# Attention's output projection in three columns at a time, its weights laid out in order of use, and new tables of turns

## The chip, the cores and the metric

The kernel runs on one core of one Trainium2 chip. The metric is device time in microseconds (us), the median of several runs. Matrix products run on TensorE (PE, with its weight loads shown as PEld), elementwise work on VectorE (DVE), ScalarE (ACT) and GpSimd (POOL); SyncE (SP), ACT and POOL also issue DMAs.

## The reference: a GLA layer, an attention layer, a gated MLP behind each

512 tokens of width 1024 go through two layers. Layer 0 mixes tokens by gated linear attention, layer 1 by softmax attention; a gated MLP with a width-3 convolution follows each. The change is in layer 1's mixer:

```python
def attn_mixer(h, w_qkv, q_norm, k_norm, w_out, cos, sin):
    ...
    q = apply_rope(rmsnorm(q, q_norm).astype(jnp.float32), cos, sin).astype(h.dtype)
    k = apply_rope(rmsnorm(k, k_norm).astype(jnp.float32), cos, sin).astype(h.dtype)
    ...
    def block(q_blk):
        s = jnp.einsum('bkgqd,bksd->bkgqs', q_blk, k).astype(jnp.float32) * scale
        p = jax.nn.softmax(s, axis=-1).astype(v.dtype)
        return jnp.einsum('bkgqs,bksd->bkgqd', p, v)
    o = lax.map(block, qb)
    o = o.transpose(1, 0, 4, 2, 3, 5).reshape(B, S, ATTN_Q_HEADS * ATTN_HEAD_DIM)
    return o @ w_out
```

There are 8 query heads and 2 key/value heads of 128; queries go in blocks of 128. The output o (512 x 1024) is multiplied by w_out (1024 x 1024) and added to x.

## The kernel before

Activations lie feature-major: x is eight tiles x[c] of 128 features x 512 tokens. Products keep float32 precision by splitting each operand into a high part and a low rest (tiles `wh`, `wl` of weights, the two halves of `xhl`, `q`, `k`, `oT`): `mm3` (line 385) issues high x high, high x low and low x high into one PSUM bank. PSUM's eight banks are pools by tag: three `acc`, two `s`, two `pt`, one `po`.

**Weights.** A class `Weights` holds a list of halves in order of use. `get` converts the next half ahead of time: SP loads 1 MB into one of two `raw` buffers, ACT copies it to `wh` (line 167), and either DVE subtracts (line 172) or ACT writes minus the high part to `wl` (line 169) and a POOL DMA adds the raw weights onto it (line 210). The `w` pool has six tiles, three halves. The first four of the eight halves of `w_aout` go by POOL's DMA, the other four by DVE.

**The turns.** The attention part works on 32 blocks (head h, query block j), one per turn t of the loop at the end of `attention`; "turn t" below is the turn in which block t's scores are issued. Turn t issues:

- `scores` of block t: 3 matmuls of 512 columns into an `s` bank, DVE's maximum `mx` (line 1060) and `nb` (line 1061), ACT's exponential `p` with its sum `sm` (line 1063);
- `copy` of block t-1: an ACT-queue DMA `pr<-p` (line 1075);
- pieces of other work that the table names for this turn;
- `turn` of block t-LAG: four PE transposes into a `pt` bank (line 1087), ACT's high part `pth` (line 1090), DVE's rest `ptl` (line 1091), which frees the bank;
- `shares` of block t: DVE's reciprocal `rc` (line 1068), ACT's scaling of `p` (line 1069);
- in every second turn `mix`, two blocks back by LAG2: 12 matmuls of 256 columns (`po`) from `pth`, `ptl` and v; after a head's second mix, `oT` is split by ACT and DVE (lines 980, 981).

LAG and LAG2 are 5 and 7. The other work has two sources. `qpair(i)`, i = 1 to 3, makes heads 2i and 2i+1: 16 steps of 3 matmuls (tiles A and B), squares (`qa`, `qb`), four rotations `rt` on DVE, a tiny product `hs` on PE whose DVE result POOL raises to a power (`qsc`), sums `ry` on POOL, and the split of `q`. `out_steps` is the output projection: for a pair of columns c it walks the heads k in steps of 6 matmuls, alternating between the two columns' banks. It does heads 0 to 5 for columns 0, 1 (`acc`) and 2, 3 (`s`), heads 6 and 7 for these, and then columns 4, 5 and 6, 7 whole. A finished column is added to x (line 449) and prepared for the MLP by `nxt.chunk`, which writes an `xhl` tile. That pool has eight tiles, and the `oT` of heads 4 to 7 lie in it too. Twelve of the 32 steps are issued in turns, from turn 22 on; the others follow the loop.

The framework then orders instructions on each engine by priority, starting from this order of issue, and assigns banks and semaphores; each engine runs its own list strictly in order. The tables therefore decide where on PE's list a piece stands between the parts of the softmax chain.

Of the kernel before, what the change touches and what calls it, by code (L numbers as in the profile page):

```python
# [13 lines left out]
ALU = mybir.AluOpType  # L14

P = 128
S = 512
D = 1024
KC = D // P
# [10 lines left out]

GATE_STEPS, GATE_LAG = (0, 2, 5, 7, 10, 12, 15, 17), 2

LAGS = (5, 7)

Q_STEPS = {1: (0, (4,) * 4), 2: (4, (3, 3, 2, 2, 2, 2, 2)), 3: (11, (2,) * 8)}
Q_READY = {1: (4, (3, 3, 2, 1, 1, 0, 1)), 2: (11, (3, 2, 2, 1, 1, 1, 0, 1)), 3: (19, (3, 2, 2, 1, 1, 1, 0, 1))}

O_STEPS = (22, 23, 25, 27, 29, 31, 32, 33, 34, 35, 36, 37)


PLAIN = 6
PARTS = (4, 4, 4, 4, 3, 3)
TILES = {4: (2, 2, 2, 2), 3: (2, 3, 3)}
# [16 lines left out]
def hybrid_encoder_kernel(  # L60
# [21 lines left out]
    pe, act, dve, pool, sync = nc.tensor, nc.scalar, nc.vector, nc.gpsimd, nc.sync  # L82
    pinned = [False]

    def mm(*a, **k):
        i = pe.matmul(*a, **k)  # L86
        if pinned[0]:
            tc.keep_in_program_order(i)
# [13 lines left out]
    def bank(tag, n):  # L102
        return pp.tile([P, S], F32, tag=tag, bufs=PS[tag], name=nm(n))
# [17 lines left out]
    x = [cp.tile([P, S], F32, name=f"x{c}") for c in range(KC)]  # L121
# [112 lines left out]
    W = Weights()  # L234
# [191 lines left out]
    def out_steps(src, hl, nxt):  # L426


        pss, ws = {}, {}

        def part(ng, ks):
            if ng not in pss:
                pss[ng] = [bank("s" if ng % 2 else "acc", "op") for _ in range(2)]
            for k in ks:
                hf, kk = divmod(k, 4)
                if (ng, hf) not in ws:
                    ws[ng, hf] = W.half(src, ng * 2 + hf)
                wh, wl = ws[ng, hf]
                for i, (wt, mv) in enumerate(((wh, hl[k][0]), (wh, hl[k][1]), (wl, hl[k][0]))):
                    for n in range(2):  # L440
                        sl = slice((kk * 2 + n) * P, (kk * 2 + n + 1) * P)
                        mm(pss[ng][n], wt[:, sl], mv, start=k == 0 and i == 0, stop=k == KC - 1 and i == 2)
                W.flush()
                yield

        def end(ng):
            for n in range(2):
                c = ng * 2 + n
                dve.tensor_tensor(x[c], x[c], pss[ng][n], ALU.add)
                nxt.chunk(c)  # L450

        yield from part(0, range(6))
        yield from part(1, range(6))
        for ng in range(2):
            yield from part(ng, (6, 7))
            end(ng)
        for ng in (2, 3):
            yield from part(ng, range(KC))
            end(ng)


    def gla(norm, nxt):
        norm.high(0)
# [451 lines left out]
    def attention(norm, nxt):  # L915
# [90 lines left out]
        def qpair(i, tag="acc"):  # L1006
            head, sc = yield from roped(1 + i, PC_QK, float(HD), "qsc", tag)
            for e in range(2):
                y = head(e)
                yield  # L1010
                t = big(F32R, "q")
                split(y, t)
                heads[2 * i + e] = (t, sc, e)
                yield
# [18 lines left out]
        ps = [bank("acc" if j < 2 else "pt", "av") for j in range(NT)]  # L1033
# [8 lines left out]
        for j in range(NT):  # L1042
            sl = slice(j * 256, (j + 1) * 256)
# [4 lines left out]
        oh = [None] * QH  # L1048
# [57 lines left out]

        LAG, LAG2 = LAGS
        blocks = [(h, j) for h in range(QH) for j in range(NT)]
        osteps = out_steps(w_aout, oh, nxt)
        plan = collections.defaultdict(list)  # L1110
        for i in range(1, QH // 2):
            g = qpair(i)
            for first, counts in (Q_STEPS[i], Q_READY[i]):
                for t, n in enumerate(counts):
                    plan[first + t] += [g] * n
        for t in O_STEPS:
            plan[t].append(osteps)
        for t in range(len(blocks) + LAG2):
            if t < len(blocks):
# [29 lines left out]
    with staged("att"):  # L1149
        attention(norms[2], norms[3])  # L1150
# [4 lines left out]
def _layout(inputs):  # L1155

    import numpy as np

    i = {k: np.asarray(v) for k, v in inputs.items()}
    con = np.ascontiguousarray  # L1160
    a = {}
    a["xT"] = con(i["x"][0].T)
    fm = lambda w: w.reshape(-1, P).T
    q, k = i["attn_q_norm"][0], i["attn_k_norm"][0]
    dup = lambda w: np.concatenate([w, w])[:, None]
    a["par"] = con(np.concatenate(
        [fm(i["norm_mix"][0]), fm(i["norm_ffn"][0]), fm(i["norm_mix"][1]), fm(i["norm_ffn"][1]),
         fm(i["gla_b_gate_f"][0]), fm(i["gla_b_gate_b"][0]),
         dup(q[:64]), dup(q[64:]), dup(k[:64]), dup(k[64:])], axis=1))
    cv = np.concatenate([i["ffn_w_conv"], i["ffn_b_conv"][:, None, :]], axis=1)  # L1170
    a["conv"] = con(cv.reshape(2, 4, 2 * FC, P).transpose(3, 0, 2, 1).reshape(P, -1))
    a["gla_norm"] = con(np.broadcast_to(i["gla_norm"][0], (P, DV)))
    wg = np.zeros((32, 1024), np.float32)
    wg[:16, :512] = i["gla_w_gate_up_f"][0]
    wg[16:, 512:] = i["gla_w_gate_up_b"][0]
    a["w_gate"] = wg
    inv = (10000.0 ** (-np.arange(32) / 32)).astype(np.float32)
    row = np.repeat(np.arange(8, dtype=np.float32), 64)
    col = np.tile(np.arange(64, dtype=np.float32), 8)
    ang = np.concatenate([row[:, None] * inv, col[:, None] * inv], axis=1).T.astype(np.float64)  # L1180
    ang = np.concatenate([ang, ang])
    a["rope"] = con(np.concatenate([np.cos(ang), np.sin(ang)], axis=1).astype(np.float32))
    sm = np.ones((P, S + 1), np.float32)
    sm[:, ::CHUNK] = 0.0
    a["scan_mask"] = sm

    w = i["gla_w_in"][0]
    ks = lambda m: m.reshape(m.shape[0] // P, P, -1)
    vg = ks(w[:, 1024:3072]).reshape(2, 4, P, 4, S)
    a["w_vg"] = con(vg.transpose(3, 0, 2, 1, 4).reshape(8, P, 4 * S))  # L1190
    a["w_r"] = con(ks(w[:, 3072:]).transpose(1, 0, 2).reshape(P, KC * 32))
    qk = ks(w[:, :1024]).reshape(KC, P, 2, GH, P)[:, :, ::-1]
    a["w_kq"] = con(qk.transpose(3, 1, 2, 0, 4).reshape(GH, P, 4 * S))

    def outw(m):
        return con(ks(m).reshape(KC, P, 4, 2, P).transpose(2, 1, 0, 3, 4).reshape(4, P, 4 * S))

    a["w_gout"] = outw(i["gla_w_out"][0])
    w = i["attn_w_qkv"][0]

    def halves(m):
        n = m.shape[1] // 256
        t = m.reshape(KC, P, n, 2, 2, 64)
        return t.transpose(2, 1, 4, 0, 3, 5).reshape(n, P, 4 * S)

    a["w_akq"] = con(np.concatenate([halves(w[:, 1024:1280]), halves(w[:, :1024])]))
    a["w_av"] = con(ks(w[:, 1280:]).transpose(1, 0, 2).reshape(1, P, 4 * S))
    a["w_aout"] = outw(i["attn_w_out"][0])
    up = i["ffn_w_up"].reshape(2, KC, P, 2, FC, P)
    a["w_up"] = con(up.transpose(0, 4, 2, 3, 1, 5).reshape(2, FC, P, 4 * S))  # L1210
    dn = i["ffn_w_down"].reshape(2, FC, P, KC, P)
    ends = np.cumsum((0,) + PARTS)
    dn = np.concatenate([dn[:, a:b].transpose(0, 3, 1, 2, 4).reshape(2, -1, P, P) for a, b in zip(ends, ends[1:])], axis=1)
    dn = dn.reshape(2, KC * FC // 16, 16, P, P)
    a["w_down"] = con(dn.transpose(0, 1, 3, 2, 4).reshape(2, -1, P, 4 * S))
    return a
# [19 lines left out]
```

## Time and profile before

| | |
|---|---|
| median of 3 runs | 1117.07 us (1115.98 to 1118.34) |
| profiled execution | 1119.08 us, span 1117.4 us |
| PE busy | 1104.9 us, 99% of the span, 6418 matmuls |
| DVE, ACT, POOL busy | 864.3, 601.0, 105.9 us |
| attention part with its turns, in the trace | about 590 to 764 us |

A busy share of PE counts each matmul from its start to its modelled end, and neighbours overlap; so short holes vanish in it, and starts have to be compared. Waits are shown by the line that waited and what released it.

### The profile page before, as it was taken

What the parts mean: (1) busy time and instruction counts of PE and PEld (TensorE: products, weight loads), DVE (VectorE), ACT (ScalarE), POOL (GpSimd) and SP (SyncE); (2) the same over time, 40 slices, a digit from 0 to 9 for tenths busy, and PEclk for the clock granted to TensorE, in tenths of its full rate; (3) what the DMA queues carried; (4) which work ended last, traced back from release to release, by engine and by line L of the source; (5) the groups of instructions that cost most, each with busy time, mean ns of one, the idle gap of its engine ahead of it and who ended that gap; (6) DMA issues with size and microseconds to landing.
All of it is one profiled execution on the core that took longest, in us unless ns stands there. A gap on an engine that the chain in (4) does not pass through costs nothing.

```text
span 1117.4 us, 16142 instructions
## 1 busy us (share of the span) xinstructions
PE 1104.9 (99%) x6418; PEld 974.1 (87%) x6418; DVE 864.3 (77%) x1325; ACT 601.0 (54%) x892; POOL 105.9 (9%) x96
## 2 busy tenths in 40 slices
PE   9999999999999999999999999999999999999998
PEld 7878888888899999999978887788879999999997
DVE  6566655459989999979885567654998999997985
ACT  6455224367645455544464788845764545544541
POOL 0213310021000000000004332101100000000000
PEclk9999999999999999999999999999999999999999
DMA  6323211368332322323337754446863232332322
GB/s 219 128 78 111 76 40 37 113 140 198 135 113 95 113 92 98 115 74 114 136 76 200 180 164 117 152 127 145 191 173 114 96 113 81 109 114 76 114 76 76
DMA packets 30938, 131.78 MB, mean 118 GB/s; under 512 B 3600, under 2 KB 4240, under 8 KB 22160
## 3 DMA queue, kind: packets, MB, share of 16 engines
q1 hardware_dynamic: 20496, 102.30, 27.5%
q0 software_dynamic: 5472, 19.93, 9.2%
q10 hardware_dynamic: 4896, 8.54, 2.1%
q8 instruction: 50, 0.82, 0.3%
q14 instruction: 24, 0.20, 0.1%
HBM read 100.34 MB, written 2.10 MB: 92 GB/s over the span
## 4 chain that ended last, share of the span: by engine, by line
PE 91%; DMA 3%; DVE 3%; ACT 2%; issue 1%; POOL 0%; SPq 0%; DVEq 0%; POOLq 0%; ACTq 0%
PE dn L86 20%; PE Y L86 16%; PE X L86 12%; PE up L86 9%; PE op L86 8%; PE vg L86 5%; PE A L86 3%; PE B L86 2%; PE po L86 2%; PE k L86 2%; PE q L86 2%; PE s L86 2%; DMA wl<-raw 2%; PE o L86 2%; PE av L86 1%
## 5 line engine op out<-in xcount | busy, mean ns | idle before, releaser
L86 PE MATMUL dn<-gu,wh 128*128 128x512 f32 x708 | 218.5, 390 | 0.8 <-DVE x L842 0.7
L86 PEld LDWEIGHTS dn<-gu,wh 128*128 128x128 f32 x708 | 130.4, 188 | 26.8 <-DVE x L842 2.1
L86 PE MATMUL dn<-gu,wl 128*128 128x512 f32 x354 | 137.4, 388 | 0.0
L86 PE MATMUL up<-xhl,wh 128*128 128x512 f32 x384 | 118.7, 390 | 0.0
L776 ACT ACTIVATE y<-u,cw 128x512 f32<-128x512 f32 x88 | 67.9, 808 | 78.4 <-DVE u L876 64.2
L167 ACT ACTIVATE wh<-raw 128x1024 fp32r<-128x1024 f32 x72 | 76.2, 1058 | 60.7 <-DVE raw L199 15.3
L86 PE MATMUL X<-th,xwh 128*128 128x256 f32 x360 | 101.9, 283 | 0.0
L86 PE MATMUL X<-th,xwl 128*128 128x256 f32 x360 | 101.9, 283 | 0.0
L86 PE MATMUL X<-tl,xwh 128*128 128x256 f32 x360 | 101.9, 283 | 0.0
L842 DVE TENSOR_TENSOR x<-x,dn 128x512 f32<-128x512 f32 x95 | 64.7, 684 | 27.9 <-PE dn L86 27.7
L167 ACT ACTIVATE wh<-draw 128x1024 fp32r<-128x1024 f32 x44 | 46.7, 1061 | 70.5 <-PE dn L86 35.5
L86 PEld LDWEIGHTS up<-xhl,wh 128*128 128x128 f32 x384 | 71.8, 188 | 14.7
L86 PE MATMUL vg<-wh,xhl 128*128 128x512 f32 x256 | 81.9, 398 | 1.4 <-DVE g L485 0.5
L210 POOL DMA_DIRECT2D wl<-raw x38 | 33.4, 878 | 515.0 <-ACT wl L169 508.7
L86 PEld LDWEIGHTS dn<-gu,wl 128*128 128x128 f32 x354 | 66.5, 188 | 13.8
L86 PE MATMUL up<-xhl,wl 128*128 128x512 f32 x192 | 75.0, 391 | 0.9 <-DMA wl<-raw 0.8
L86 PE MATMUL Y<-th,wh 128*128 128x256 f32 x264 | 74.7, 283 | 0.0
L86 PE MATMUL Y<-tl,wh 128*128 128x256 f32 x264 | 74.7, 283 | 0.0
L86 PE MATMUL Y<-th,wl 128*128 128x256 f32 x264 | 74.7, 283 | 0.0
L86 PE MATMUL op<-oT,wh 128*128 128x512 f32 x256 | 72.2, 395 | 0.0
L86 PEld LDWEIGHTS X<-th,xwh 128*128 128x128 f32 x360 | 69.0, 192 | 0.8 <-DVE v L856 0.7
L86 PEld LDWEIGHTS X<-tl,xwh 128*128 128x128 f32 x360 | 69.1, 192 | 0.1
(232 smaller groups left out, 2810.9 us busy)
## 6 DMA issues: line engine op xcount, KB each, us to landing
raw<-in_w_up_dram SPq DMA_DIRECT2D x44, 1024.0 KB, 5.0
draw<-in_w_down_dram SPq DMA_DIRECT2D x44, 512.0 KB, 3.8
wl<-raw POOLq DMA_DIRECT2D x38, 512.0 KB, 5.8
pr<-p ACTq DMA_DIRECT2D x32, 256.0 KB, 2.9
raw<-in_w_vg_dram SPq DMA_DIRECT2D x6, 1024.0 KB, 5.0
raw<-in_w_akq_dram SPq DMA_DIRECT2D x5, 1024.0 KB, 6.6
raw<-in_w_kq_dram SPq DMA_DIRECT2D x4, 1024.0 KB, 4.9
raw<-in_w_gout_dram SPq DMA_DIRECT2D x4, 1024.0 KB, 4.9
```

The source lines that it names most:

```text
L86: i = pe.matmul(*a, **k)
L167: act.activation(hi, r, AF.Copy)
L210: pool.dma_start(dst, src, accum_op=ALU.add)
L776: act.activation(yt, ut, AF.Identity, scale=w(1), bias=w(3))
L842: dve.tensor_tensor(x[c], x[c], ps, ALU.add)
```

## The change

The change replaces the two lags and all tables of turns, and gives the attention layer's output projection a generator of its own, `out_stream`. Its unit is one block of 128 x 128 weights: one head k, one column c, 3 matmuls in a row on one bank. `out_blocks` lists the 64 units: heads 0 to 5 for columns 0 to 2 (`acc`), head by head; heads 0 to 5 for column 3, then 4 (`s`); heads 6 and 7 for columns 0 to 2, then for 3 and 4; last columns 5, 6, 7, one after the other. The layout of `w_aout` in memory follows the list, 8 units to a half, so that each half is read once from front to back. A column is added to x and handed to `nxt.chunk` as soon as it is complete. The GLA layer keeps `out_steps`. The lists of SP and POOL stay as they were; PE still has the same number of matmuls, ACT and DVE the same instructions in another order.

```diff
-LAGS = (5, 7)
-
-Q_STEPS = {1: (0, (4,) * 4), 2: (4, (3, 3, 2, 2, 2, 2, 2)), 3: (11, (2,) * 8)}
...
-O_STEPS = (22, 23, 25, 27, 29, 31, 32, 33, 34, 35, 36, 37)
+LAGS = (4, 5)
+
+Q_AT = {1: (2, 2, 2, 2, 2, 2, 2, 2, 2, 2, 2, 2, 3, 3, 3, 3, 4, 4, 4, 5, 5, 5, 6, 6, 7, 8, 10),
...
+O_AT = (18, 18, 18, 18, 19, 22, 22, 23, 23, 26, 27, 28, 29, 32, 32, 32, 32, 33, 37, 37, 37, 37, 37, 37, 38, 38, 38, 38, 38, 38)
...
+    def out_blocks():
+
+        first, second, third = range(3), range(3, 5), range(5, KC)
+        return ([(k, c) for k in range(6) for c in first] + [(k, c) for c in second for k in range(6)]
+                + [(k, c) for k in (6, 7) for c in first] + [(k, c) for c in second for k in (6, 7)]
+                + [(k, c) for c in third for k in range(KC)])
+
+    def out_stream(src, hl, nxt):
+        ps, w = {}, None
+        for u, (k, c) in enumerate(out_blocks()):
+            if u % 8 == 0:
+                w = W.half(src, u // 8)
+            if c not in ps:
+                ps[c] = bank("s" if 3 <= c < 5 else "acc", "op")
+            sl = slice((u % 8) * P, (u % 8 + 1) * P)
+            mm3(ps[c], w[0][:, sl], w[1][:, sl], *hl[k], k == 0, k == KC - 1)
+            W.flush()
+            if k == KC - 1:
+                dve.tensor_tensor(x[c], x[c], ps[c], ALU.add)
+                nxt.chunk(c)
+            yield
...
-        osteps = out_steps(w_aout, oh, nxt)
+        osteps = out_stream(w_aout, oh, nxt)
         plan = collections.defaultdict(list)
         for i in range(1, QH // 2):
             g = qpair(i)
-            for first, counts in (Q_STEPS[i], Q_READY[i]):
-                for t, n in enumerate(counts):
-                    plan[first + t] += [g] * n
-        for t in O_STEPS:
+            for t in Q_AT[i]:
+                plan[t].append(g)
+        for t in O_AT:
             plan[t].append(osteps)
```

PE's list, turns 27 and 28 and the start of turn 29, before: `s_6631`, `s_6662` and `s_6698` are the scores of these three turns, `op` is the projection, `oT` a head's output.

```order
L86 MATMUL s_6631<-k_5411,q_6501 128x512 x3
L1087 MATMUL pt_6653<-ident,pr_6499 128x128 x4
L86 MATMUL s_6662<-k_5411,q_6604 128x512 x3
L1087 MATMUL pt_6676<-ident,pr_6533 128x128 x4
L86 MATMUL op_6450<-oT_6628,wh_6452 128x512
L86 MATMUL op_6451<-oT_6628,wh_6452 128x512
L86 MATMUL s_6698<-k_5411,q_6604 128x512
```

The same place now, from turn 27's scores `s_6673`; eight more rows of this mix, four transposes and the scores of turn 28 follow.

```order
L84 MATMUL s_6673<-k_5411,q_6495 128x512 x3
L84 MATMUL op_6337<-oT_6603,wh_6333 128x512
L84 MATMUL op_6337<-oT_6603,wl_6334 128x512
L84 MATMUL op_6342<-oT_6603,wh_6333 128x512
L84 MATMUL po_6660<-pth_6580,vh_5565 128x256
L84 MATMUL op_6342<-oT_6603,wl_6334 128x512
L84 MATMUL op_6346<-oT_6603,wh_6333 128x512
L84 MATMUL op_6346<-oT_6603,wl_6334 128x512
L84 MATMUL po_6660<-ptl_6581,vh_5565 128x256
L84 MATMUL po_6660<-pth_6580,vl_5566 128x256
```

Turn 27 held one group of transposes between two scores; it now holds six projection matmuls and a whole mix. Over turns 18 to 30 the list before has 39 `s`, 30 `op`, 2 B, 84 `po`, 13 groups of four transposes and one `hs`; now 39 `s`, 48 `op`, 72 `po`, 13 groups and one `hs`. On ACT the same turns hold 13 times the chain's three instructions, four weight conversions, `qa` and `qb` both times, and of `q` and `oT` splits 7 before and 5 now.

DVE's list around the last `hs`, that of `qpair(3)`, before; `rc_6376` belongs to turn 20, `mx_6411` to turn 21.

```order
L954 SCALAR_TENSOR_TENSOR rt_6346<-A_6015,prm,rope_5235 128x512
L933 SCALAR_TENSOR_TENSOR hs_6354<-hs_6349,eps 128x8
L954 SCALAR_TENSOR_TENSOR rt_6345<-B_6016,prm,rope_5235 128x512
L1068 RECIPROCAL rc_6376<-sm_6375 128x1
L1060 TENSOR_REDUCE mx_6411<-s_6407 128x1
```

And now; `rc_6384` belongs to turn 19, `mx_6418` to turn 20.

```order
L974 SCALAR_TENSOR_TENSOR rt_6330<-A_6018,prm,rope_5235 128x512
L953 SCALAR_TENSOR_TENSOR hs_6396<-hs_6391,eps 128x8
L974 SCALAR_TENSOR_TENSOR rt_6329<-B_6019,prm,rope_5235 128x512
L1111 TENSOR_TENSOR ptl_6354<-pt_6355,pth_6353 128x4x128
L974 SCALAR_TENSOR_TENSOR rt_6331<-B_6019,prm,rope_5235 128x512
L1088 RECIPROCAL rc_6384<-sm_6383 128x1
L1080 TENSOR_REDUCE mx_6418<-s_6414 128x1
```

The reciprocal behind `hs` has two instructions more in front of it, and belongs to a turn earlier. On PE the product `hs` that it waits for stood behind the scores of turn 21, and now stands behind those of turn 20.

More of the change, by code (lines that the diff above doesn't have):

```diff
@@ L31 @@
 GATE_STEPS, GATE_LAG = (0, 2, 5, 7, 10, 12, 15, 17), 2
-LAGS = (5, 7)
-Q_STEPS = {1: (0, (4,) * 4), 2: (4, (3, 3, 2, 2, 2, 2, 2)), 3: (11, (2,) * 8)}
-Q_READY = {1: (4, (3, 3, 2, 1, 1, 0, 1)), 2: (11, (3, 2, 2, 1, 1, 1, 0, 1)), 3: (19, (3, 2, 2, 1, 1, 1, 0, 1))}
-O_STEPS = (22, 23, 25, 27, 29, 31, 32, 33, 34, 35, 36, 37)
+LAGS = (4, 5)
+Q_AT = {1: (2, 2, 2, 2, 2, 2, 2, 2, 2, 2, 2, 2, 3, 3, 3, 3, 4, 4, 4, 5, 5, 5, 6, 6, 7, 8, 10),
+        2: (4, 4, 4, 5, 5, 5, 6, 6, 7, 7, 7, 7, 9, 9, 11, 11, 12, 12, 12, 12, 12, 13, 13, 13, 14, 15, 17),
+        3: (11, 11, 11, 13, 14, 14, 14, 14, 14, 14, 16, 16, 17, 17, 17, 17, 18, 18, 19, 19, 19, 20, 21, 21, 22, 24, 26)}
+O_AT = (18, 18, 18, 18, 19, 22, 22, 23, 23, 26, 27, 28, 29, 32, 32, 32, 32, 33, 37, 37, 37, 37, 37, 37, 38, 38, 38, 38, 38, 38)
 PLAIN = 6
@@ L1207, in _layout @@
     a["w_av"] = con(ks(w[:, 1280:]).transpose(1, 0, 2).reshape(1, P, 4 * S))
-    a["w_aout"] = outw(i["attn_w_out"][0])
+    m = i["attn_w_out"][0].reshape(KC, P, KC, P)
+    order = ([(k, c) for k in range(6) for c in range(3)] + [(k, c) for c in (3, 4) for k in range(6)]
+             + [(k, c) for k in (6, 7) for c in range(3)] + [(k, c) for c in (3, 4) for k in (6, 7)]
+             + [(k, c) for c in range(5, KC) for k in range(KC)])
+    m = np.stack([m[k, :, c] for k, c in order]).reshape(4, 16, P, P)
+    a["w_aout"] = con(m.transpose(0, 2, 1, 3).reshape(4, P, 4 * S))
     up = i["ffn_w_up"].reshape(2, KC, P, 2, FC, P)
```

## The prediction

> **What bounds the kernel now.** I read the page first, busy shares and the chain that ended last.
>
> ```profile
> PE 1104.9 (99%) x6418; PEld 974.1 (87%) x6418; DVE 864.3 (77%) x1325; ACT 601.0 (54%) x892; POOL 105.9 (9%) x96
> ...
> PE 91%; DMA 3%; DVE 3%; ACT 2%; issue 1%; POOL 0%; SPq 0%; DVEq 0%; POOLq 0%; ACTq 0%
> ```
>
> PE sets the time, and the change leaves PE the same matmuls. It can only gain where PE stands still or runs at a lower clock, and lose where it makes new holes. So I cut the attention part into stretches: busy time of PE, PEld, DVE, ACT, POOL, then PE's granted clock.
>
> ```profile
> 619.00:683.00 64.00, 64.00 (x362) 54.66 (x361) 38.00 (x92) 52.20 (x95) 19.73 (x17) 1.00 0.62 173
> 683.00:715.00 32.00, 27.80 (x165) 22.96 (x164) 23.81 (x53) 27.24 (x52) 8.65 (x7) 0.95 0.49 148
> 715.00:737.00 22.00, 22.00 (x145) 19.45 (x144) 10.90 (x21) 12.87 (x23) 0.86 (x1) 1.00 0.40 120
> ```
>
> All holes lie in 32 us, turns 20 to 28: 4.2 us idle, and a clock of 0.95, which is 32 x 0.05 = 1.6 us. The waits of PE there:
>
> ```profile
> PE pt L1087 <- issue: 1.4, 1, 1.4
> PE pt L1087 <- PE s L86: 0.9, 2, 0.7
> PE s L86 <- DVE q L981: 0.9, 2, 0.5
> PE s L86 <- ACT p L1063: 0.5, 1, 0.5
> PE po L86 <- DVE rc L1068: 0.3, 1, 0.3
> PE s L86 <- ACT q L980: 0.3, 1, 0.3
> ```
>
> These eight waits make the 4.2 us, and all end on the softmax chain: scores wait for a bank that ACT's exponential reads, or for a split q; transposes wait for a `pt` bank. PE's own spacing shows what each hole costs beyond the idle time:
>
> ```profile
> 678.66 0.86 PE L86 MATMUL s<-k,q 128*128 128x512 f32 x3
> ...
> 701.29 0.46 PE L1087 MATMUL pt<-ident,pr 128*128 128x128 f32 x4
> 701.58 0.35 PE L86 MATMUL po<-pth,vh 128*128 128x256 f32 x1
> ...
> 703.31 0.28 PE L86 MATMUL po<-pth,vh 128*128 128x256 f32 x1
> 703.43 0.28 PE L86 MATMUL po<-ptl,vh 128*128 128x256 f32 x1
> ...
> 718.24 0.86 PE L86 MATMUL s<-k,q 128*128 128x512 f32 x3
> ...
> 762.43 1.07 PE L86 MATMUL op<-oT,wh 128*128 128x512 f32 x4
> ...
> 763.79 0.61 PE L86 MATMUL up<-xhl,wh 128*128 128x512 f32 x2
> 764.24 0.39 PE L86 MATMUL up<-xhl,wl 128*128 128x512 f32 x1
> 764.47 0.61 PE L86 MATMUL up<-xhl,wh 128*128 128x512 f32 x2
> ```
>
> Six projection matmuls that alternate between two banks take 763.79 - 762.43 = 1.36, 0.227 each; three on one bank 764.47 - 763.79 = 0.68, also 0.227. One is booked as 0.39 and so hides 0.16 behind each hole: 8 x 0.16 = 1.3. The loss is then 4.2 + 1.3 + 1.6 = 7.1 us. A second count: a 256-column matmul costs 0.12 and four transposes 0.29. Turns 18 to 30 hold, by the order, 71 matmuls of 512 columns, 84 of 256, 13 groups of transposes and an `hs` of about 0.8: 16.1 + 10.1 + 3.8 + 0.8 = 30.8 us. They ran from 678.66 (scores of 18) to 718.24 (scores of 31), 39.6 us: 8.8 lost. I take 8.0.
>
> **Why PE ran dry.** ACT's costs, start to start:
>
> ```profile
> 678.89 0.78 ACT L1063 ACTIVATE p<-s,nb,qsc 128x512 f32<-128x512 f32 x1
> ...
> 679.66 0.59 ACT L1090 ACTIVATE pth<-pt 128x512 fp32r<-128x512 f32 x1
> 680.14 0.72 ACT L1069 ACTIVATE p<-p,rc 128x512 f32<-128x512 f32 x1
> 680.83 0.78 ACT L1063 ACTIVATE p<-s,nb,qsc 128x512 f32<-128x512 f32 x1
> ...
> 681.60 0.62 ACT L980 ACTIVATE q<-ry 128x512 fp32r<-128x512 f32 x1
> 682.12 0.59 ACT L1090 ACTIVATE pth<-pt 128x512 fp32r<-128x512 f32 x1
> ...
> 720.12 0.78 ACT L1063 ACTIVATE p<-s,nb,qsc 128x512 f32<-128x512 f32 x1
> ```
>
> ```profile
> 672.38 1.05 ACT L167 ACTIVATE wh<-raw 128x1024 fp32r<-128x1024 f32 x1
> 673.33 1.05 ACT L169 ACTIVATE wl<-raw 128x1024 fp32r<-128x1024 f32 x1
> ```
>
> A bare turn costs ACT 680.83 - 678.89 = 1.94, a q, `oT`, `qa` or `qb` about 0.52, a conversion 0.95. Turns 18 to 30: 13 x 1.94 + 4 x 0.95 + 9 x 0.52 = 33.7 us of ACT against 30.8 of PE. PE has too little else to do there and follows ACT, and from 680.83 to 720.12 (39.3 us) ACT itself stood still for 5.6. Its largest late item:
>
> ```profile
> 686.88 0.78 ACT L1063 ACTIVATE p<-s,nb,qsc 128x512 f32<-128x512 f32 x1
> ...
> 689.50 0.17 DVE L933 SCALAR_TENSOR_TENSOR hs<-hs,eps 128x8 f32<-128x8 f32 x1 [0.73 <-PE hs L86]
> 689.58 0.74 DVE L954 SCALAR_TENSOR_TENSOR rt<-B,prm,rope 128x512 f32<-128x512 f32 x1
> 690.24 0.15 DVE L1068 RECIPROCAL rc<-sm 128x1 f32<-128x1 f32 x1
> ...
> 691.22 0.73 ACT L1069 ACTIVATE p<-p,rc 128x512 f32<-128x512 f32 x1
> ```
>
> The exponential ends at 687.66, its reciprocal comes at 690.24, because DVE waits in its list for the tiny product `hs`, which PE issues only behind the next scores. About 2.5 us of ACT go there.
>
> **The change part by part.**
>
> *Projection pieces moved forward.* PE's list now holds for turns 18 to 30: 87 x 0.227 + 72 x 0.12 + 3.8 + 0.8 = 32.9 us. ACT's: 25.2 + 3.8 + 7 x 0.52 = 32.6. A shortage of 2.9 becomes a surplus of 0.3. The places agree: turn 27, 0.97 us of PE work before (three scores, four transposes), now has 0.97 + 6 x 0.227 + 12 x 0.12 = 3.8. That is the gain.
>
> *The `hs` wait.* It stays, one turn earlier, and two more instructions (a rotation, a `ptl`, 0.7 each) stand between `hs` and the reciprocal: 2.5 + 1.4 = 3.9 us late instead of 2.5. Behind it queue ACT's scaling and exponential, and so scores two turns on. The cover is the ten projection matmuls of turn 20 and what precedes them. An exponential ends 680.83 + 0.77 - 678.66 = 2.9 after its scores start; its bank is needed two turns later, 2 x 32.9/13 = 5.1. So PE feels no ACT lag below 2.2 us.
>
> *What is left of the holes.* ACT needs 32.6 plus its own idle time. With idle time from 0.3 (no loss) to 5.6 (as before), and 0 to 2.2 of lag given away at the end of the stretch, PE waits between 0 and 32.6 + 5.6 - 32.9 = 5.3. I take 3.9 from `hs` plus 0.6: 32.6 + 4.5 - 2.2 - 32.9 = 2.0, rounded up to 2.2 for single handovers.
>
> *Shorter lags.* Transposes come four instead of five turns behind the scores, a mix one turn behind its transposes instead of two. Costed in the first rival; nothing in the forecast.
>
> *One column at a time, three banks.* The spacing above is the same for one bank or two: nothing. The weight halves are read front to back, three in the pool, by unchanged SP and POOL lists. One of them is near: the second half's addition by POOL stands behind `qsc`, 1.66 us, which follows `hs`.
>
> ```profile
> 689.82 1.66 POOL L935 TENSOR_TENSOR qsc<-hs,halfneg 128x8 f32<-128x8 f32 x1 [14.23 <-DVE hs L933]
> ...
> wl<-raw POOLq DMA_DIRECT2D x38, 512.0 KB, 5.8
> ```
>
> From the start of turn 20's scores: `hs` starts at 0.7, `qsc` 1.3 later and done at 3.7, landing 5.8 later at 9.5. The first user stands in turn 23, after PE work of 4.4 + 2.9 + 1.9 + 0.9 = 10.1. Hidden by 0.6 us; if the landing is 2 us later than this median, 1.4 show. I take nothing, and keep 1.4 for the range.
>
> *The end.* Columns 5 to 7 now finish singly.
>
> ```profile
> L357 DVE SCALAR_TENSOR_TENSOR xhl<-x,prm,xhl x8: 745/750/755, 741.6 to 767.5; 128x512 fp32r<-128x512 f32 x8
> ```
>
> Before, the last `xhl` rest began at 767.5 and ended at 768.25; its user, the eighth step of `up`, was due at 763.79 + 7 x 0.68 = 768.55. Two columns stood before it at the end, now one, so it is earlier. Nothing, either way.
>
> *Sum.* The profiled execution took 1119.08 us, 2.0 above the median of the runs; its holes stand for theirs. 1119.08 - 8.0 + 2.2 = 1113.3 in a profiled execution, 1117.07 - 8.0 + 2.2 = 1111.3 in the median.
>
> **The rivals.**
>
> *Slower: the shorter lag shows.* A mix waits for `pth` (0.59) and `ptl` (0.7) of the transposes one turn back, with handovers about 1.9. Turn 28 now holds only scores and transposes, 0.97, so the transposes that end turn 27 have 0.97 + 0.68 = 1.7 us until the mix of turn 29. If ACT still has a scaling and an exponential ahead (0.7 + 0.8 = 1.5), that mix waits about 1.4. It decides from the point where ACT runs over 1.5 us late through the stretch; then five mixes, turns 21 to 29, pay 7.0, and the 3.9 of `hs` is uncovered: 1117.07 - 8.0 + 7.0 + 3.9 = 1120.0. For it speaks that ACT and PE are within 0.3 us of each other; against it, most of these turns keep projection pieces in front of the mix.
>
> *No change that shows: ACT binds as before.* With its old idle time of 5.6, PE waits 5.3, and a slow stretch of the clock comes back for 1.6: 1117.07 - 8.0 + 6.9 = 1116.0; without the clock 1114.4.
>
> *The clock stays slow.* The rows give a clock of 0.95 in the stretch whose longest wait is 1.4 us; if these holes did not cause it, 1.6 us of the gain stay out: 1112.9. [...] The trace speaks against it so far, since the clock is 1.00 in the neighbouring stretches without holes.
>
> *The change does nothing.* Excluded: PE's list differs at the places named.
>
> **How the numbers follow.** Forecast 0.58, from 1108.8 (8.8 regained, 0.5 of new waits) to 1113.6 (7.1 regained, 2.2 and the late landing's 1.4 lost); slow clock 0.08, ACT binds 0.22 (a quarter of it below 1114.8), lag shows 0.12. A measurement here can tell 0.2%, 2.2 us, from no change: bounds 1114.8 and 1119.3. Faster 0.58 + 0.08 + 0.05 = 0.71, same 0.17, slower 0.12. For 8 in 10 the range takes in 1116.0 with the late landing, 1117.4, and leaves out the slower rival: 1108.8 to 1117.4.
>
> **What would show it.** Right: between turns 18 and 31 PE idles under about 1.5 us, the clock is 1.00, ACT's idle time falls below 5 us, and the stretch from the scores of turn 18 to those of turn 31 shrinks from 39.6 to about 35. Wrong: waits of `po` on `ptl` or `pth` (lag), of `s` on `p` in every turn (ACT), of `op` on `wl` (landing), or new holes before turn 18, which the table for `qpair` moves too and which had none.

## The result, and the profile after

The changed kernel takes 1110.96 us (median of 6 runs, 1109.69 to 1112.53) beside 1117.70 of the kernel before (6 runs): a ratio of 0.9942, 95% interval 0.993 to 0.9955. Measured again later it gave 1110.76 (6 runs), ratio 0.9939 (0.9919 to 0.9958). So the gain is 6.5 us, 0.6%. The profiled execution took 1111.09 us, with a span of 1109.4 instead of 1117.4.

The page of the changed kernel, busy shares and the chain that ended last:

```profile
PE 1099.3 (99%) x6418; PEld 971.5 (88%) x6418; DVE 864.4 (78%) x1325; ACT 599.8 (54%) x892; POOL 104.7 (9%) x96
...
PE 90%; DVE 4%; DMA 3%; ACT 2%; issue 1%; POOL 0%; SPq 0%; DVEq 0%; POOLq 0%; ACTq 0%
```

PE does the same 6418 matmuls; its busy time, in which matmuls at a clock of 0.50 count longer (before, a 256-column `po` is booked with 0.41 us at 712 us and with 0.28 at 717), is 5.6 us lower, and the span 8.0. The same three stretches as before (us, PE, PEld, DVE, ACT, POOL, granted clock, DMA):

```profile
619.00:683.00 64.00, 64.00 (x363) 54.65 (x361) 39.42 (x93) 50.91 (x94) 19.65 (x16) 1.00 0.59 166
683.00:715.00 32.00, 31.54 (x203) 27.59 (x202) 24.40 (x58) 29.21 (x58) 8.61 (x7) 1.00 0.53 157
715.00:737.00 22.00, 22.00 (x133) 19.22 (x132) 12.07 (x18) 12.70 (x20) 0.86 (x1) 1.00 0.48 156
```

In the middle row PE idled 4.2 us at a clock of 0.95; it now idles 0.46 at 1.00. The first row, which holds the turns up to 18 and their new query table, has no idle time, as before. Of the waits between 590 and 770 us one is left (line numbers of the changed file: matmuls L84 instead of L86, the rest some 20 higher):

```profile
PE po L84 <- DVE ptl L1111: 0.5, 1, 0.5
```

Now the path from the first scores to the MLP, on PE:

```profile
616.45 1.09 PE L84 MATMUL s<-k,q 128*128 128x512 f32 x4
...
678.26 0.93 PE L84 MATMUL s<-k,q 128*128 128x512 f32 x3
...
713.39 0.85 PE L84 MATMUL s<-k,q 128*128 128x512 f32 x3
...
754.44 0.62 PE L84 MATMUL up<-xhl,wh 128*128 128x512 f32 x2
```

and the first scores of the kernel before:

```profile
619.11 0.86 PE L86 MATMUL s<-k,q 128*128 128x512 f32 x3
```

Scores of turn 18 to scores of turn 31: 713.39 - 678.26 = 35.1 us instead of 39.6, although the stretch holds 32.9 us of PE work instead of 30.8. So 2.2 us are lost there instead of 8.8: 6.6 regained, as much as the medians differ by. From the first scores to the first matmul of `up`: 754.44 - 616.45 = 137.99 instead of 763.79 - 619.11 = 144.68, 6.7 us less. The spans differ by 8.0, since two differences lie outside: the turns began 619.11 - 616.45 = 2.7 us earlier, and the MLP took 1.35 longer, for a wait treated below. The 2.7 are no work of the change: both kernels issue the same 3456 matmuls before the first scores, and 2.3 us of the 2.7 arise in the first 14 us. Four `vg` matmuls there take 9.15 - 7.45 = 1.70 us in this execution of the kernel before,

```profile
7.45 1.91 PE L86 MATMUL vg<-wl,xhl 128*128 128x512 f32 x4
9.15 2.77 PE L86 MATMUL vg<-wh,xhl 128*128 128x512 f32 x8
```

and 7.59 - 6.68 = 0.91 in this one of the changed kernel:

```profile
6.68 1.08 PE L84 MATMUL vg<-wl,xhl 128*128 128x512 f32 x4
7.59 2.06 PE L84 MATMUL vg<-wh,xhl 128*128 128x512 f32 x8
```

The clock column reads 1.00 there for both, so what slowed them stays open. In the 14 profiles the first scores start anywhere from 616.15 to 619.11 us.

### The profile page after: what moved, and what is told of

Same layout as the page of the kernel before. It is cut to its first block, busy times and chain, and to the rows that moved or that the text cites. A ratio compares the mean times of both kernels' runs of the same rounds, so it can differ in the third digit from the quotient of the medians.

```text
span 1109.4 us, 16149 instructions
## 1 busy us (share of the span) xinstructions
PE 1099.3 (99%) x6418; PEld 971.5 (88%) x6418; DVE 864.4 (78%) x1325; ACT 599.8 (54%) x892; POOL 104.7 (9%) x96
## 4 chain that ended last, share of the span: by engine, by line
PE 90%; DVE 4%; DMA 3%; ACT 2%; issue 1%; POOL 0%; SPq 0%; DVEq 0%; POOLq 0%; ACTq 0%
PE dn L84 21%; PE Y L84 17%; PE X L84 12%; PE op L84 8%; PE up L84 8%; PE vg L84 5%; PE A L84 3%; PE B L84 2%; PE po L84 2%; PE s L84 2%; PE k L84 2%; PE q L84 2%; PE o L84 2%; DMA wl<-raw 1%; PE av L84 1%; PE kv L84 1%
## 5 line engine op out<-in xcount | busy, mean ns | idle before, releaser
L84 PE MATMUL dn<-gu,wh 128*128 128x512 f32 x708 | 218.7, 390 | 0.8 <-DVE x L862 0.7
L84 PEld LDWEIGHTS dn<-gu,wh 128*128 128x128 f32 x708 | 130.5, 188 | 26.6 <-DVE x L862 2.1
L84 PE MATMUL dn<-gu,wl 128*128 128x512 f32 x354 | 137.5, 388 | 0.0
L84 PE MATMUL up<-xhl,wh 128*128 128x512 f32 x384 | 118.8, 391 | 0.0
L84 PE MATMUL X<-th,xwh 128*128 128x256 f32 x360 | 102.1, 284 | 0.0
L84 PE MATMUL X<-th,xwl 128*128 128x256 f32 x360 | 102.0, 283 | 0.0
L84 PE MATMUL X<-tl,xwh 128*128 128x256 f32 x360 | 102.0, 283 | 0.0
L84 PEld LDWEIGHTS up<-xhl,wh 128*128 128x128 f32 x384 | 71.9, 188 | 14.7
L84 PE MATMUL vg<-wh,xhl 128*128 128x512 f32 x256 | 80.4, 392 | 1.8 <-DVE wh L216 1.0
L84 PEld LDWEIGHTS dn<-gu,wl 128*128 128x128 f32 x354 | 66.6, 188 | 13.8
L84 PE MATMUL up<-xhl,wl 128*128 128x512 f32 x192 | 75.1, 391 | 1.8 <-DMA wl<-raw 1.8
L84 PE MATMUL op<-oT,wh 128*128 128x512 f32 x256 | 76.1, 394 | 0.0
L84 PE MATMUL Y<-th,wl 128*128 128x256 f32 x264 | 74.8, 283 | 0.0
L84 PE MATMUL Y<-th,wh 128*128 128x256 f32 x264 | 74.8, 283 | 0.0
L84 PE MATMUL Y<-tl,wh 128*128 128x256 f32 x264 | 74.8, 283 | 0.0
L84 PEld LDWEIGHTS X<-th,xwh 128*128 128x128 f32 x360 | 69.2, 192 | 0.8 <-DVE v L876 0.7
L84 PEld LDWEIGHTS X<-tl,xwh 128*128 128x128 f32 x360 | 69.2, 192 | 0.1
```

## The experiments

Each kernel ran several times beside the kernel before; the column ratio compares these runs. "Turns" is the profiled time from the first scores to the first `up`, worked out from the starts of these two rows as above; the idle times of PE are 20 minus its busy time in two 20-us windows of one profiled execution. "Half clock" counts the runs whose mean clock was 0.998 or less: the four profiles with such a mean have one 20-us window at 0.83 to 0.91 between 680 and 720, the ten others read 1.00 there; the three of the four that were read more closely hold a stretch at 0.50 (last section). Gains in us are one minus the ratio, times 1117; the ratio is not exactly the quotient of the two medians.

| kernel | median, us | ratio (95% interval) | turns | idle 680-700 | idle 700-720 | half clock |
|---|---|---|---|---|---|---|
| before | 1117.16 | 1 | 144.7 | 2.2 | 2.0 | 53 of 85 |
| changed, both times | 1110.96, 1110.76 | 0.9942, 0.9939 | 138.0, 137.9 | 0.0 | 0.5 | 0 of 12 |
| changed, old lags | 1115.44 | 0.9985 (0.9976-0.9995) | 141.5 | 1.8 | 1.0 | 4 of 11 |
| changed, two columns | 1113.72 | 0.9973 (0.9963-0.9983) | 141.2 | 0.5 | 2.1 | 1 of 12 |
| before, new lags | 1114.62 | 0.9981 (0.9970-0.9992) | 141.2 | 0.8 | 1.3 | 0 of 9 |
| before, new projection | 1115.68 | 0.9988 (0.9979-0.9997) | 144.1 | 1.9 | 1.5 | 1 of 11 |
| changed, old query turns | 1116.26 | 1.0001 (0.9988-1.0013) | 141.6 | 1.8 | 1.0 | 8 of 12 |
| changed, lags (4, 7) | 1114.82 | 0.9981 (0.9972-0.9991) | 141.9 | 1.7 | 0.7 | 8 of 12 |
| changed, lags (4, 6) | 1114.33 | 0.9976 (0.9964-0.9987) | 139.9 | 0.4 | 1.2 | 3 of 12 |
| changed, late table | 1113.46 | 0.9970 (0.9959-0.9981) | 141.0 | 0.3 | 2.0 | 0 of 12 |
| old lags, `hs` later | 1116.56 | 0.9983 (0.9970-0.9996) | 144.8 | 1.9 | 1.0 | 3 of 12 |
| changed, more ACT | 1111.83 | 0.9944 (0.9925-0.9963) | 138.7 | 0.0 | 0.8 | 0 of 6 |
| changed, last tile by DVE | 1110.35 | 0.9933 (0.9913-0.9954) | 138.0 | 0.0 | 0.5 | 0 of 6 |

A profiled execution is one draw from its kernel's runs. Ratios decide about the time; the windows tell where.

### Is it the projection's pieces, the lags or the query table?

My theory was the prediction's: projection pieces fill turns 18 to 30. The first rival said that the shorter chain is what counts, the second the query table. Four kernels undo or do one part.

```diff
-LAGS = (4, 5)
+LAGS = (5, 7)
```

> The changed kernel with the lags of before, (5, 7). Turns 18 to 30 then hold 45 projection matmuls, 33.4 us of PE work against 33.2 of ACT. Filling theory (the gain comes from projection pieces that stand in turns 18 to 30): nearly the whole gain stays, 1110 to 1113.5 us. Lag theory (the gain comes from the chain ending earlier): 1115 us or more. Table theory (the gain comes from where the pieces of the query projection stand): 1110 to 1112.

Measured 0.9985, only 1.7 us below before, so the old lags cost (0.9985 - 0.9942) x 1117 = 4.8 us. The filling and the table theory missed; the lag theory held. Of these 4.8 us the profiled execution shows 3.5 between the first scores and `up` (141.5 instead of 138.0), and 1.7 of them in one wait. PE's row with the largest wait and the rows ahead of it:

```profile
681.14 0.35 PE L84 MATMUL po<-pth,vh 128*128 128x256 f32 x1
...
682.51 0.28 PE L84 MATMUL po<-pth,vl 128*128 128x256 f32 x1
682.63 1.55 PE L84 MATMUL s<-k,q 128*128 128x512 f32 x6
685.87 1.02 PE L84 MATMUL hs<-bd,qa 128*128 128x2 f32 x8 [1.69 <-DVE qa L966]
```

The same place in the changed kernel, with DVE's `ptl` for the mix that follows:

```profile
680.69 0.68 DVE L1111 TENSOR_TENSOR ptl<-pt,pth 128x512 fp32r<-128x512 f32 x1
...
680.71 0.93 PE L84 MATMUL s<-k,q 128*128 128x512 f32 x3
...
681.71 0.28 PE L84 MATMUL po<-pth,vh 128*128 128x256 f32 x1
...
683.48 0.28 PE L84 MATMUL po<-pth,vl 128*128 128x256 f32 x1
683.60 0.86 PE L84 MATMUL s<-k,q 128*128 128x512 f32 x3
684.29 0.95 PE L84 MATMUL hs<-bd,qa 128*128 128x2 f32 x8
```

Both lists have a mix (twelve `po`, 1.4 us), the scores of turns 19 and 20, and `hs`. With the old lags the mix stands first, and PE has nothing between these six scores and `hs`. With the new ones `ptl` is done only at 681.37, after the scores of turn 19 could start, and the mix stands behind them: PE has it and three projection matmuls (0.7 us) to do until 683.60, while DVE gets through the maximum of turn 19, a rotation and `qa`. `hs` then starts without a wait.

```diff
-        first, second, third = range(3), range(3, 5), range(5, KC)
+        first, second, third = range(2), range(2, 4), range(4, KC)
```

> The changed kernel with the projection in columns 0 and 1, then 2 and 3, then 4 to 7, still one block of weights at a time, in the new layout, with new lags and the new table for the query projection. Two columns of the five heads ready hold at most 30 matmuls: turns 18 to 30 then have 32 projection matmuls instead of 48, 29.0 us of PE work against 32.7 of ACT. Filling theory: the loss of before returns, 1115 to 1119 us, and PE idles over 3 us between turns 18 and 31. Lag theory and table theory: the gain stays, 1110 to 1112.

Only the line on the columns is shown. The bank rule and the layout of `w_aout` follow it, and the projection's table was adapted too: up to turn 30 it loses the entry of turn 19, and 28 and 29 become 29 and 30. So columns and table change together here.

Measured 0.9973, 3.5 us above the changed kernel and 3.0 below before, between the ranges of the theories: each was half right. In the two windows PE idles 2.5 us, not the 3 and more that the filling theory wanted. The early place stays good (0.5 us idle), the later one is as bad as before:

```profile
680.00:700.00 20.00, 19.54 (x125) 16.76 (x124) 17.12 (x38) 18.62 (x38) 7.75 (x6) 1.00 0.55 168
700.00:720.00 20.00, 17.92 (x114) 15.27 (x115) 14.12 (x33) 18.74 (x38) 0.87 (x1) 1.00 0.44 136
```

The same two windows with the old lags and three columns, the other way round:

```profile
680.00:700.00 20.00, 18.16 (x117) 15.42 (x116) 15.16 (x35) 17.24 (x34) 7.74 (x6) 1.00 0.53 168
700.00:720.00 20.00, 19.05 (x122) 16.26 (x122) 14.12 (x35) 17.60 (x35) 0.88 (x1) 1.00 0.39 119
```

So there are two losses. The later one, turns 25 to 29, comes back when the third column goes. How much of it the moved table entries cost was not tested, and the table alone can cost as much (the late table below, 3.1 us).

```diff
-LAGS = (5, 7)
+LAGS = (4, 5)
```

in the kernel before, and nothing else:

> The kernel before with the new lags (4, 5) and nothing else. 32 projection matmuls in turns 18 to 30, 29.3 us of PE work against 32.1 of ACT. Filling theory: no gain, 1115 to 1120 us (above 1118 if transposes one turn before their mix show as waits on pth and ptl). Lag theory: 1110 to 1112.

Measured 0.9981, 2.1 us gained: less than the lag theory wanted, but the filling theory had none. Both ranges were missed, that of the filling theory by 0.4 us.

The projection alone: the changed kernel with old lags and the old query turns, written in the new form of the table.

```diff
-LAGS = (4, 5)
+LAGS = (5, 7)
...
+Q_AT = {1: (0, 0, 0, 0, 1, 1, 1, 1, 2, 2, 2, 2, 3, 3, 3, 3, 4, 4, 4, 5, 5, 5, 6, 6, 7, 8, 10),
...
```

> The three columns with their layout and table alone: lags (5, 7) and the query projection's turns as before. 45 projection matmuls in turns 18 to 30, 33.9 us of PE work against 34.6 of ACT. Filling theory: most of the gain, 1110.5 to 1114 us. Lag theory and table theory: 1115 to 1118.

Measured 0.9988, 1.3 us gained: 1.7 above the filling theory's range, and inside that of the other two. Fifteen more projection matmuls stand in turns 18 to 30 than before, yet the turns take 144.1 us instead of 144.7. They left most of the holes open: in the two windows PE idles 3.4 us, where the kernel before idles 4.2.

### What of the lags and of the tables?

After these four I took up an evenness theory: time is lost where one turn of PE's list is much longer than the next.

Four kernels change one table or lag of the changed kernel. The query turns of before, alone:

```diff
+Q_AT = {1: (0, 0, 0, 0, 1, 1, 1, 1, 2, 2, 2, 2, 3, 3, 3, 3, 4, 4, 4, 5, 5, 5, 6, 6, 7, 8, 10),
...
```

> The changed kernel with the query projection's turns of before: new lags, three columns, new table for the projection. 48 projection matmuls in turns 18 to 30, 32.9 us of PE work, 34.1 of ACT. But PE's list is lumpy: turns 20 to 23 hold 0.7, 1.4, 6.0 and 5.9 us, where the changed kernel has 4.0, 2.9, 1.9 and 4.0. Evenness theory (formed after the first four runs: in turns 18 to 30 ACT sets the pace, and loses it where one turn of PE's list is much longer than another, since scores then come late): most of the gain is gone, 1113 to 1116 us, ACT idle over 4 us between the exponentials of turns 18 and 31. Filling theory as predicted (the number of projection matmuls decides): 1111 to 1112.5. Lag theory: 1111 to 1112.5.

Measured 1.0001: no gain left by the ratio, 0.9 us by the medians (1117.13 for the runs beside it), although lags and columns are new. The evenness theory put it at 1113 to 1116, and it is 1116.26; the filling and the lag theory, at 1111 to 1112.5, missed. In 8 of 12 runs the mean clock is 0.998 or less, with a median of 1118.32 us; the other four have 1115.45, so the clock is a part of this loss. PE waits 1.4 us at `hs` again:

```profile
683.61 0.28 PE L82 MATMUL po<-pth,vl 128*128 128x256 f32 x1
683.73 0.86 PE L82 MATMUL s<-k,q 128*128 128x512 f32 x3
684.99 0.96 PE L82 MATMUL s<-k,q 128*128 128x512 f32 x3 [0.41 <-ACT p L1081]
...
687.37 1.02 PE L82 MATMUL hs<-bd,qa 128*128 128x2 f32 x8 [1.42 <-DVE qa L964]
```

The mix still stands between the scores of turns 19 and 20, but with the old table `hs` comes a turn later, behind the scores of turn 21, and nothing stands between these and the scores of turn 20. So a short mix lag is not enough: it is the query table that puts `hs` one group of scores behind the mix, and not two. The query table is as necessary as the rest.

The old lag of the mix, alone:

```diff
-LAGS = (4, 5)
+LAGS = (4, 7)
```

> The changed kernel with lags (4, 7): transposes early as in the change, mixes late as before. 41 projection matmuls in turns 18 to 30, 32.5 us of PE work, 33.2 of ACT; turns 19 to 22 hold 0.7, 5.4, 1.0 and 3.6 us of PE work. Evenness theory: 1113.5 to 1116 us, with a wait of PE on hs or scores in turns 19 to 21. Lag theory in the form that early transposes matter: 1110.5 to 1112. In the form that early mixes matter: 1114 to 1116, as with both lags old.

Measured 0.9981, about as with both lags old, and the same hole. The evenness theory and the form of the lag theory in which early mixes matter both held. Its longest waits in the turns:

```profile
PE hs L84 <- DVE qa L966: 1.7, 1, 1.7
PE pt L1107 <- DMA pr<-p: 0.5, 1, 0.5
```

So with a mix lag of 7 it makes no difference that can be told whether the transposes come four or five turns behind. A transpose lag of 5 with a mix lag of 5 or 6 was not run. All five kernels with a mix lag of 7 idle 1.7 to 2.2 us between 680 and 700; so does the kernel with the old query turns (1.8), whose mix lag is 5.

One turn more for the mix:

```diff
-LAGS = (4, 5)
+LAGS = (4, 6)
```

> The changed kernel with lags (4, 6): each mix two turns behind its transposes, in odd turns instead of even. 45 projection matmuls in turns 18 to 30, 32.0 us of PE work against 31.2 of ACT, no turn over 4.1 us. Evenness theory: as the changed kernel, 1109.5 to 1112.5 us, ACT idle under 3.5 us, and no wait of po on ptl. Lag theory (shorter is better): 1112 to 1114.

Measured 0.9976, 1.8 us above the highest that the evenness theory gave and 0.3 above that of the lag theory. The early place is good, no `po` waits for `ptl`, but transposes wait three times, 1.5 us in all, and in 3 of 12 runs the mean clock is 0.998 or less. Evenness as I counted it does not predict the time.

The projection's table begun later, with 18 entries instead of 30; the other pieces follow the loop:

```diff
-O_AT = (18, 18, 18, 18, 19, 22, 22, 23, 23, 26, 27, 28, 29, 32, 32, 32, 32, 33, 37, 37, 37, 37, 37, 37, 38, 38, 38, 38, 38, 38)
+O_AT = (27, 27, 27, 28, 28, 28, 29, 29, 29, 30, 30, 30, 31, 31, 32, 32, 32, 33)
```

> The changed kernel with the table of the projection's turns begun at turn 27 instead of 18. The order that comes out holds 46 projection matmuls in turns 18 to 30 instead of 48 and differs in few turns (turn 18 1.4 instead of 2.3 us, turn 20 1.7 instead of 4.0, turn 21 4.2 instead of 2.9). That the projection's table matters: 1113 us or more. That it hardly does, since pieces that are ready are put in front wherever PE would wait: 1110.5 to 1112.5.

Measured 0.9970, 3.1 us above the changed kernel, so the projection's table matters, though PE's list differs in few turns. One cause shows in the trace and is not PE's order: the pieces also ask for their weights. ACT's conversion of the third half, which was

```profile
696.58 1.06 ACT L165 ACTIVATE wh<-raw 128x1024 fp32r<-128x1024 f32 x1
```

in the changed kernel, comes here at 713.20, and PE waits for it:

```profile
713.20 1.06 ACT L165 ACTIVATE wh<-raw 128x1024 fp32r<-128x1024 f32 x1
...
720.09 0.73 PE L84 MATMUL op<-oT,wl 128*128 128x512 f32 x2 [1.21 <-DMA wl<-raw]
```

With another of 0.29 at 694.44, for the second half, PE waits 1.5 us for weights; the rest of the 3.1 was not traced.

### Is `hs` the hole?

In the version with old lags, the step of the last query pair that issues `hs` and the two behind it were moved a turn later:

```diff
-        3: (11, 11, 11, 13, 14, 14, 14, 14, 14, 14, 16, 16, 17, 17, 17, 17, 18, 18, 19, 19, 19, 20, 21, 21, 22, 24, 26)}
+        3: (11, 11, 11, 13, 14, 14, 14, 14, 14, 14, 16, 16, 17, 17, 17, 17, 18, 18, 20, 20, 20, 20, 21, 21, 22, 24, 26)}
```

> The changed kernel with the old lags (5, 7), and the tiny product hs of the last query pair a turn later (step 19 of its table at turn 20 instead of 19, with the next step). Hole theory (the old lags cost what the hole of PE in front of hs costs, 1.7 us of waiting plus the clock that falls after it): 1113 to 1114 us, 1.5 to 2.5 below the version with old lags alone. Evenness theory: turns 19 and 20 hold 1.0 and 3.6 us instead of 0.7 and 5.4, so a gain too, to 1112.5 to 1114. Lag theory (old lags cost by themselves): no gain, 1115 to 1116.

Measured 0.9983 against 0.9985: no gain, a miss for hole and evenness theory. The wait has only changed its name. Scores of turns 19 and 20, then

```profile
682.59 0.93 PE L84 MATMUL s<-k,q 128*128 128x512 f32 x3
685.41 0.73 PE L84 MATMUL op<-oT,wh 128*128 128x512 f32 x2 [1.89 <-DVE rt L974]
```

a projection matmul, which waits for a rotation on DVE to free its bank. Both pieces that stood there, `hs` and this one, wait for an instruction late on DVE's list; of the mix's operands DVE makes only `ptl`, which is done earlier (681.37 in the changed kernel).

### Does ACT set the pace?

```diff
             act.activation(p, p, AF.Copy, scale=rc)
+            if t >= 18 and t % 2 == 0:
+                act.activation(p, p, AF.Copy)
```

> The changed kernel with seven more instructions on ACT in the even turns 18 to 30: a copy of the scaled p onto itself behind the scaling, 0.6 us each, 4.2 us in all; it computes nothing new. ACT sets the pace of these turns in the changed kernel too: 2.5 to 4.2 us longer than it, 1113.5 to 1115.5. PE sets the pace and ACT has its idle 3 us to give: under 1.5 us longer, 1111 to 1112.5.

Measured 0.9944 against 0.9939, or 1111.83 us against 1110.76: 0.6 to 1.1 us for 4.2 us of ACT. ACT does not set the pace in the changed kernel. The stretch from the scores of turn 18 to those of turn 31:

```profile
678.65:715.18 36.53, 35.73 (x225) 30.79 (x224) 27.79 (x63) 35.55 (x71) 8.61 (x7) 1.00 0.49 147
```

ACT is busy for 35.55 of 36.53 us: it has given its idle time. The stretch is 1.4 us longer, and part of that is PE work which the order put there (51 projection matmuls instead of 48, 0.7 us).

### The wait behind the turns

```diff
-BY_DMA = (5, 6)
+BY_DMA = (5, 5)
```

The numbers say how many weight tiles of each layer's `up` product POOL's DMA finishes; DVE finishes the others.

> The changed kernel with the two halves of the sixth weight tile of the last MLP's up product finished by DVE instead of by POOL's DMA. PE waited for that DMA for 0.7 to 1.5 us once or twice near 800 and 813 us in every kernel so far, 1.8 in the changed one. If that wait goes: 0.7 to 1.8 us faster than the changed kernel. If DVE, which has more to do there, takes its place, or the wait moves to the tile before: within 0.5.

Measured 0.9933 against 0.9939, with intervals that overlap: not told apart from the changed kernel. The wait of `up` went, and another came in the MLP:

```profile
PE dn L84 <- DVE wl L170: 0.8, 1, 0.8
```

Beside these last three ran the changed kernel itself:

> The changed kernel unaltered, beside the other three and more runs of the kernel before. If its lead of 6.7 us is real it is again 1110 to 1112 us, 5.5 to 7 below the kernel before; if part of it was the draw of six runs, 1112 to 1114. The clock should stay at 1.00 in all runs.

It repeated its lead, and its trace repeats the first within 0.1 us from the first scores to `up`.

## Why the prediction was right, and where it was not

**The size and place of the loss: right.** 8.8 us were lost between the scores of turns 18 and 31; 2.2 are lost now. Forecast were 8.0 regained and 2.2 new waits, a gain of 5.8 and 1111.3 us; measured are a gain of 6.5 and 1110.96. The agreement of the medians is the one to trust: that of the profiled executions contains 2.7 us from before the turns. Part of it is luck. PE's waits now make 0.5 us, 0.6 with what a hole hides, not 2.2; and by the same count, of waits, of what holes hide and of the clock, 7.1 had been lost, not 8.0. The two errors pull in opposite directions, and -7.1 + 0.6 is the measured 6.5. The 8.8 and the 2.2 of the other count both hold 1.6 to 1.7 us that are neither waits nor clock, so that its 2.2 are not the forecast's new waits.

**ACT's idle time: right.** From the exponential of turn 18 to that of turn 31 ACT now stands still for 35.28 - 32.49 = 2.8 us, where it was 39.29 - 33.84 = 5.5 (the prediction says 5.6).

**The cause: half right.** The step that failed is that a shortage of PE work against ACT's, 2.9 us, becomes a surplus of 0.3, and that this is the gain. The balance is not enough: with old lags it was as good (33.4 to 33.2), and 4.8 us were lost; 4.2 us more of ACT cost 0.6 to 1.1. By the traces, what counts is which piece stands at the two places where PE would wait: in turns 19 to 21 a mix, together with a query table that puts `hs` one group of scores behind it; in turns 25 to 29 projection pieces of a third column. The second is the filling that I forecast, up to 3.5 us by the two-column kernel, whose table moved too.

**Shorter lags, "nothing in the forecast": wrong.** They are worth 2.1 us alone and 4.8 beside the other parts. I costed them only as a danger. Of that rival, mixes that wait for `ptl` one turn back, one wait of 0.46 came, not five of 1.4.

**`hs` one turn earlier and 3.9 us late: too much.** The exponential of turn 19 and its reciprocal:

```profile
685.26 0.82 ACT L1083 ACTIVATE p<-s,nb,qsc 128x512 f32<-128x512 f32 x1
685.93 0.24 ACT L1083 ACTIVATION_READ_ACCUMULATOR p<-s,nb,qsc 128x1 f32 x1
...
687.56 0.71 ACT L1089 ACTIVATE p<-p,rc 128x512 f32<-128x512 f32 x1
```

```profile
685.28 0.17 DVE L953 SCALAR_TENSOR_TENSOR hs<-hs,eps 128x8 f32<-128x8 f32 x1 [0.75 <-PE hs L84]
...
687.27 0.16 DVE L1088 RECIPROCAL rc<-sm 128x1 f32<-128x1 f32 x1
```

It comes at 687.27, 1.2 us behind the exponential's end at 686.08: the exponential was itself late, behind two squares and two conversions on ACT, and met a DVE that had passed `hs`. The prediction also counted only the scores two turns on that this delay could hold up. It left out that PE itself can wait at `hs`, for `qa` from DVE: the projection matmuls of turn 20, which it named as cover, stand behind `hs` on PE's list and cover nothing of that wait; the mix ahead of it does. With the old lags that wait is 1.7 us, and the first projection matmul behind `hs` (685.87) starts at 686.75.

**The clock: 1.6 us per execution that has it, but not all have.** Of 85 runs of the kernel before, 53 had a mean clock of 0.998 or less, median 1117.93 us; the other 32 had 1116.13. Of 12 runs of the changed kernel none had. So the clock is worth 1.8 x 53/85 = 1.1 us of the difference of medians, as an estimate, and the waits the other 5.4. The rival that the clock stays slow falls; so do ACT binding as before, and a change that does nothing.

**Nothing for POOL's landing, the banks and the end: right.** No projection matmul waits for `wl` in the turns, and none at the end.

**Not foreseen:** `up` waits for POOL's DMA in the last MLP 1.8 us instead of 0.8. The other kernels that keep this DMA show 0.7 to 1.7, and the repeat of the changed kernel 1.2, so much of the difference may be chance.

**Left open:** what the query table does alone, beyond the place of `hs` in one trace; how much of the later place the third column fills and how much its table; and the interplay that makes it worth 6.6 us (1.0001 against 0.9942) beside the others, where the two-column kernel with it and the new lags alone without it differ by 0.9, with intervals that overlap.

## What to carry to other kernels

A balance of two engines' work over a stretch tells whether holes can be filled, not whether they are; look for what stands ahead of each waiting instruction on its own list: here the pieces behind `hs` covered nothing of its wait of 1.69 us with the old lags. Undo the parts of a change one by one before crediting one of them: here each undone part took back about half of the gain or more. A lag of a software pipeline is also a choice of place: one turn less put a block of work behind the scores instead of in front of them.

## What the runs showed of the hardware

In three profiles the granted clock read 0.50 for some us right behind a stretch with holes. The kernel before, three neighbouring windows around the slow stretch (the number behind POOL's time is the clock):

```profile
707.10:710.50 3.40, 2.31 (x12) 1.48 (x13) 2.96 (x8) 3.40 (x9) 0.00 (x0) 1.00 0.91 244
710.55:713.94 3.39, 3.39 (x15) 3.14 (x14) 1.67 (x5) 2.95 (x6) 0.00 (x0) 0.50 0.37 138
713.96:717.36 3.40, 3.40 (x24) 2.96 (x23) 2.30 (x5) 1.72 (x4) 0.00 (x0) 1.00 0.17 64
```

PE was busy for 2.31 of 3.40 us, its longest wait 0.72, and the next 3.4 us ran at 0.50. The version with lags (4, 7) had a wait of 1.7 us and was busy for 1.98 of 3.40, and its next 3.40 us ran at 0.50. The version with old lags and `hs` later ran at 0.50 for 6.81 us after its wait of 1.9:

```profile
682.98:686.40 3.42, 1.53 (x7) 0.96 (x6) 3.38 (x7) 3.42 (x7) 0.86 (x1) 1.00 0.30 57
686.44:693.25 6.81, 6.81 (x26) 6.02 (x25) 3.14 (x9) 1.72 (x4) 2.61 (x2) 0.50 0.89 263
693.27:696.68 3.41, 3.41 (x24) 2.98 (x23) 1.53 (x4) 2.13 (x5) 3.20 (x4) 1.00 0.10 32
```

The version with old lags alone had a wait of 1.7 us too and was busy for 1.73 of 3.42, yet its next 3.40 us ran at 1.00 in the profiled execution, so a hole did not always bring the stretch. By the neighbours at 1.00, the stretch of the kernel before is between 3.39 and 3.46 us long, and that with `hs` later between 6.81 and 6.87. What sets these lengths, and why only some runs have a stretch, was not shown. In the kernel before no single wait was long: the slow stretch came behind four of at most 0.72 us, 1.5 us in all.
